# The last four rows of a logsumexp loaded as four uneven runs of columns, with VectorE adding up their parts

## The chip, the cores and the metric

The kernel runs on one core of a Trainium2 chip. The metric is device time in microseconds (us), the median of several runs on the same chip. A profile is one more execution, recorded by the hardware profiler; its times are given from the start of its span.

## The reference

```python
def setup_inputs():
    batch, seq, dim = 32, 512, 1024
    return {
        "x": np.random.randn(batch, seq, dim).astype(np.float32),
        "axis": -1,
    }

def reference(x: np.ndarray, axis: int) -> np.ndarray:
    x_max = np.max(x, axis=axis, keepdims=True)
    return (x_max.squeeze(axis) + np.log(np.sum(np.exp(x - x_max), axis=axis))).astype(np.float32)
```

A logsumexp over the last axis: 16,384 rows of 1024 fp32 numbers (67.1 MB) come in, 16,384 numbers (65.5 KB) go out.

## The kernel before

**Layout.** The 16,384 rows are spread over the 128 partitions, 128 rows to a partition (`x_v`, `NB = 128`); below, "a row" means one row of 1024 columns on every partition, 512 KB in all. A ring of 51 rows in SBUF (`ring`) takes them in.

**Optimistic pass.** The kernel does not subtract the maximum first. It takes exp of the raw numbers, sums each row, takes the logarithm of the sums and stores that. It then counts, with a compare against two bounds (`LOW`, `HIGH`) and two small matmuls over the partitions, whether every sum lay between 1e-18 and 1e18. If one did not, a second pass (`second_pass`, `second_vector`) does the whole work again with the maximum subtracted; with this input it is not entered. So the program ends when the verdict has been read and branched on and both stores of the result have landed (the last wait, on `stored`).

**Loads.** `CHUNKS` lists 17 loads, all issued in order by SyncE (SP) in `load(i)`: 4, 15, 16, 16, 16, 14, 13, 9, 7, 5, 4, 3, 2 rows and then four single rows. I number them from 1. A load into ring slots that were used before waits on counters of VectorE (`dve_done`) and ScalarE (`act_done`) until these slots are free. Load 1 is moved ahead of the opening barrier.

**Work on a load.** Each entry of `CHUNKS` is (rows, rows that VectorE sums, parts, by halves). ScalarE waits for the load, takes exp in place over all rows of a part in one instruction (L235), and VectorE sums them: either with one reduction over the part (L255), or, where `by halves` is set, row by row with `tensor_tensor_reduce` (L242), which adds the right half of the row to the left half and accumulates the sum in the same instruction, so that 512 steps do for 1024 columns. The rows that VectorE does not sum are done by ScalarE alone, one row at a time with `accum_out` (L262): an ACTIVATE and then an instruction that reads the accumulator out.

**The end.** The last four rows (`LATE = 4`) are single loads whose sums ScalarE accumulates into PSUM (`late`; L262 for three of them, L225 for the last). Logarithms (L162) are taken in three goes: 81 rows when load 7 is done, 43 rows just before the last row, and the last four. Two stores follow: 124 columns of the result (L276, 496 bytes to a partition), waiting for the second of these, and 4 columns (L278, 16 bytes), waiting for the third. VectorE takes the maximum and minimum of the first 124 sums (L293, L294), compares them and then the four late sums with the bounds (L283, twice), TensorE counts (L304, L307, 6 columns), VectorE sums the counts into `verdict` (L312), and SyncE, VectorE and ScalarE read it and branch.

**Waits.** An instruction carries one wait of its own. Where the program asks for two before an instruction, the one asked for first stays with it and the other becomes an instruction of its own that only waits, just ahead.

Of the kernel before, what the change touches and what calls it, by code (L numbers as in the profile page):

```python
# [7 lines left out]


CHUNKS = [  # L10
    (4, 4, 1, False), (15, 15, 1, False), (16, 16, 2, False), (16, 16, 2, False),
    (16, 15, 2, False), (14, 14, 2, False), (13, 12, 2, False), (9, 8, 1, False),
    (7, 7, 1, True), (5, 4, 1, True), (4, 3, 1, True), (3, 3, 1, False), (2, 2, 1, True),
    (1, 0, 1, False), (1, 0, 1, False), (1, 0, 1, False), (1, 0, 1, False),
]

CUTS = ()
RING_ROWS = 51


UNEVEN = ()
PARTS = ((0, 128, 2), (1, 128, 4), (3, 128, 8), (7, 64, 8), (71, 128, 8))


LN_AT = 7
LN_LAG = 1


LATE = 4


LOW, HIGH = 1e-18, 1e18
# [6 lines left out]
def kernel(  # L39
# [6 lines left out]
    nc = tc.nc  # L46
    P = nc.NUM_PARTITIONS
# [4 lines left out]
    N, D = x_flat.shape  # L52
    assert N % P == 0
    NB = N // P
    assert sum(r for r, *_ in CHUNKS) == NB
    assert sum(STEPS) == NB

    fp32, bf16, int32 = mybir.dt.float32, mybir.dt.bfloat16, mybir.dt.int32
    Exp = mybir.ActivationFunctionType.Exp
    Ln = mybir.ActivationFunctionType.Ln  # L60
    Alu = mybir.AluOpType
    AX = mybir.AxisListType.X

    x_v = x_flat.rearrange("(p t) d -> p t d", p=P)
    out_v = bass.AP(tensor=out.tensor, offset=out.offset, ap=[[NB, P], [1, NB]])


    assert CHUNKS[-1][0] == 1
    spans = list(zip((0, *CUTS), (*CUTS, D)))
    assert 1 <= len(spans) <= 2  # L70
    n_late = LATE - 1 + len(spans)

    K = 2 + n_late

    ring = nc.alloc_sbuf_tensor("ring", [P, RING_ROWS, D], fp32).ap()
    sums = nc.alloc_sbuf_tensor("sums", [P, NB], fp32).ap()
    res = nc.alloc_sbuf_tensor("res", [P, NB], fp32).ap()
    bounds = nc.alloc_sbuf_tensor("bounds", [P, 2, K], fp32).ap()
    above = nc.alloc_sbuf_tensor("above", [P, 2, K], bf16).ap()
    ends = nc.alloc_sbuf_tensor("ends", [P, 2], fp32).ap()  # L80
    weights = nc.alloc_sbuf_tensor("weights", [P, 2], bf16).ap()
    verdict = nc.alloc_sbuf_tensor("verdict", [1, 1], int32).ap()
    peak = nc.alloc_sbuf_tensor("peak", [P, NB], fp32).ap()
# [1 line left out]
    late = nc.alloc_psum_tensor("late", [P, 512], fp32).ap()  # L85

    ALL_GOOD = P * K
    TOO_MANY = 2048.0
    assert TOO_MANY > ALL_GOOD

    landed = [nc.alloc_semaphore(f"landed{i}") for i in range(len(CHUNKS) + len(spans) - 1)]
    act_done = nc.alloc_semaphore("act_done")
    dve_done = nc.alloc_semaphore("dve_done")
    pool_done = nc.alloc_semaphore("pool_done")
# [22 lines left out]

    place = []
    row = slot = 0
    for r, *_ in CHUNKS:  # L120
        if slot + r > RING_ROWS:
            slot = 0
        place.append((slot, row))
        slot += r
        row += r
# [6 lines left out]
        ends = [-(-n * k // parts) for k in range(parts + 1)]  # L132
        return [(lo, hi) for lo, hi in zip(ends, ends[1:]) if lo < hi]

    def load(i):
        (s, row), r = place[i], CHUNKS[i][0]
        act_wait = max(a for a, _ in busy[s : s + r])
        dve_wait = max(d for _, d in busy[s : s + r])
        if dve_wait:
            nc.sync.wait_ge(dve_done, dve_wait)  # L140
        if act_wait:
            nc.sync.wait_ge(act_done, act_wait)
        dst, src = ring[:, s : s + r], x_v[:, row : row + r]
        if i == len(CHUNKS) - 1:
            for k, (lo, hi) in enumerate(spans):
                nc.sync.dma_start(out=dst[:, :, lo:hi], in_=src[:, :, lo:hi]).then_inc(
                    landed[i + k], 16
                )
        elif i in UNEVEN:
            for first, last, step in PARTS:  # L150
                nc.sync.dma_start(
                    out=dst[first:last:step], in_=src[first:last:step]
                ).then_inc(landed[i], 16)
        else:
            nc.sync.dma_start(out=dst, in_=src).then_inc(landed[i], 16)

    def take_logs(lo, hi, src, dve_wait, act_wait, bias=0.0):
        nonlocal acts
        nc.scalar.wait_ge(act_done, act_wait)
        if dve_wait:  # L160
            nc.scalar.wait_ge(dve_done, dve_wait)
        nc.scalar.activation(out=res[:, lo:hi], in_=src, func=Ln, bias=bias).then_inc(  # L162
            act_done, 1
        )
        acts += 1

    late_row = place[-LATE][1]
    assert not any(n_dve for _, n_dve, _, _ in CHUNKS[-LATE:])

    def total(t):  # L170
        return late[:, t - late_row : t - late_row + 1] if t >= late_row else sums[:, t : t + 1]

    body = nc.main_func.blocks[-1]
    n_barrier = len(body.instructions)
# [33 lines left out]
    nc.gpsimd.memset(weights[:, :1], 1.0)  # L208
    nc.gpsimd.memset(weights[:, 1:], -TOO_MANY).then_inc(pool_done, 1)

    logged = 0
    done_before = [(0, 0)]
    for i, (r, n_dve, parts, by_halves) in enumerate(CHUNKS):
        if i:
            load(i)
        s, row = place[i]
        if i == LN_AT:
            logged = place[i - LN_LAG][1]
            take_logs(0, logged, sums[:, :logged], *done_before[i - LN_LAG])
        if i == len(CHUNKS) - 1:  # L220
            take_logs(logged, late_row, sums[:, logged:late_row], *done_before[-LATE])
            early_logs = acts
            for k, (lo, hi) in enumerate(spans):
                nc.scalar.wait_ge(landed[i + k], 16)
                nc.scalar.activation(  # L225
                    out=ring[:, s, lo:hi],
                    in_=ring[:, s, lo:hi],
                    func=Exp,
                    accum_out=late[:, LATE - 1 + k : LATE + k],
                ).then_inc(act_done, 1)  # L230
                acts += 1
            continue
        nc.scalar.wait_ge(landed[i], 16 * (len(PARTS) if i in UNEVEN else 1))
        for lo, hi in cuts(n_dve, parts):
            nc.scalar.activation(  # L235
                out=ring[:, s + lo : s + hi], in_=ring[:, s + lo : s + hi], func=Exp
            ).then_inc(act_done, 1)
            acts += 1
            nc.vector.wait_ge(act_done, acts)
            if by_halves:  # L240
                for j in range(lo, hi):
                    nc.vector.tensor_tensor_reduce(  # L242
                        out=ring[:, s + j, : D // 2],
                        in0=ring[:, s + j, : D // 2],
                        in1=ring[:, s + j, D // 2 :],
                        scale=1.0,
                        scalar=0.0,
                        op0=Alu.add,
                        op1=Alu.add,
                        accum_out=sums[:, row + j : row + j + 1],  # L250
                    ).then_inc(dve_done, 1)
                    dves += 1
                    busy[s + j] = (0, dves)
            else:
                nc.vector.reduce_sum(  # L255
                    out=sums[:, row + lo : row + hi], in_=ring[:, s + lo : s + hi], axis=AX
                ).then_inc(dve_done, 1)
                dves += 1
                for j in range(lo, hi):
                    busy[s + j] = (0, dves)  # L260
        for j in range(n_dve, r):
            nc.scalar.activation(  # L262
                out=ring[:, s + j],
                in_=ring[:, s + j],
                func=Exp,
                accum_out=total(row + j),
            ).then_inc(act_done, 1)
            acts += 1
            busy[s + j] = (acts, 0)
        done_before.append((dves, acts))  # L270

    take_logs(late_row, NB, late[:, : NB - late_row], dves, acts)


    nc.sync.wait_ge(act_done, early_logs)
    nc.sync.dma_start(out=out_v[:, :late_row], in_=res[:, :late_row]).then_inc(stored, 16)  # L276
    nc.sync.wait_ge(act_done, acts)
    nc.sync.dma_start(out=out_v[:, late_row:], in_=res[:, late_row:]).then_inc(stored, 16)  # L278


    def compare(lo, hi, values):
        nonlocal dves
        nc.vector.tensor_tensor(  # L283
            out=above[:, :, lo:hi],
            in0=values.unsqueeze(1).to_broadcast([P, 2, hi - lo]),
            in1=bounds[:, :, lo:hi],
            op=Alu.is_gt,
        ).then_inc(dve_done, 1)
        dves += 1

    nc.vector.wait_ge(act_done, done_before[-LATE][1])
    nc.vector.wait_ge(dve_done, dves)
    nc.vector.reduce_max(out=ends[:, :1], in_=sums[:, :late_row], axis=AX).then_inc(dve_done, 1)  # L293
    nc.vector.tensor_reduce(  # L294
        out=ends[:, 1:], in_=sums[:, :late_row], axis=AX, op=Alu.min
    ).then_inc(dve_done, 1)
    dves += 2
    nc.vector.wait_ge(pool_done, 1)
    nc.vector.wait_ge(dve_done, dves)
    compare(0, 2, ends)  # L300
    nc.vector.wait_ge(act_done, acts)
    compare(2, K, late[:, :n_late])
    nc.tensor.wait_ge(dve_done, dves)
    nc.tensor.matmul(  # L304
        votes[:1, :K], lhsT=weights[:, :1], rhs=above[:, 0], start=True, stop=False
# [90 lines left out]
```

## Time and profile before

| | us |
|---|---|
| median of 3 runs (lowest, highest) | 162.49 (162.25, 162.52) |
| the profiled execution, its own time | 162.67 |
| span of its trace | 161.3 |
| DVE (VectorE) busy | 121.9 |
| ACT (ScalarE) busy | 115.1 |
| bytes read from HBM | 67.11 MB, 416 GB/s over the span |

The largest groups of instructions, with their number, busy time and mean length:

| line, engine | what | number | busy us | mean ns |
|---|---|---|---|---|
| L255 DVE | sums of a part, one reduction | 14 | 111.2 | 7994 |
| L235 ACT | exp of a part | 18 | 104.4 | 5836 |
| L242 DVE | sum of a row by halves | 16 | 9.9 | 684 |
| L262 ACT | exp and sum of one row | 8 | 8.2 | 1041 |

The engines' busy times are averages over stages with different limits. Two instructions on one engine overlap a little in the trace (the end of one and the start of the next), so the distance from start to start of two that follow each other without a wait is what one costs, and it is a little shorter than the duration shown.

### The profile page before, as it was taken

The page shows a single profiled execution, that of the slowest core. Times are in us where ns is not written, and L with a number is a line of the kernel's source. Part 1 is how long each engine was busy: PE and PEld are TensorE (multiplying, and loading weights), DVE is VectorE, ACT ScalarE, POOL GpSimd, SP SyncE. Part 2 cuts the span into 40 slices and gives each one's busy share as a digit, 9 for nine tenths or more (in the row PEclk, how much of TensorE's full clock was granted, in tenths as well). Part 3 has the DMA queues.
Part 4 walks back from the last instruction along what each step waited for, and adds up shares of the span by engine and source line. Part 5 has one row for each costly group of instructions (what it writes and reads, how often), then busy time and mean ns, then how long its engine had stood idle before and what let it go on. Part 6 is the DMA issues. An engine that isn't in the chain of part 4 may idle for free.

```text
span 161.3 us, 149 instructions
## 1 busy us (share of the span) xinstructions
PE 0.2 (0%) x2; PEld 0.1 (0%) x2; DVE 121.9 (76%) x51; ACT 115.1 (71%) x40; POOL 0.4 (0%) x8
## 2 busy tenths in 40 slices
PE   0000000000000000000000000000000000000000
PEld 0000000000000000000000000000000000000000
DVE  0028000003999999999999699999999999999884
ACT  3170005996079960999419993999199999999996
POOL 1000000000000000000000000000000000000000
DMA  7999799979979989989979999999999999999991
GB/s 256 508 488 442 305 472 520 439 341 520 439 341 520 423 358 520 423 358 520 423 325 455 455 455 439 423 423 423 412 402 430 436 420 410 427 436 412 417 407 42
DMA packets 2737, 67.18 MB, mean 417 GB/s; under 512 B 560, under 2 KB 560, under 8 KB 1072
## 3 DMA queue, kind: packets, MB, share of 16 engines
q1 hardware_dynamic: 2736, 67.18, 97.4%
q14 instruction: 1, 0.01, 0.0%
HBM read 67.11 MB, written 0.07 MB: 416 GB/s over the span
## 4 chain that ended last, share of the span: by engine, by line
DMA 49%; DVE 30%; ACT 20%; issue 0%; PE 0%
DMA ring<-in_x_dram 49%; DVE sums L255 29%; ACT ring L235 17%; ACT ring L262 3%; ACT ring L225 1%; ACT res L162 0%; DVE above L283 0%; PE votes L304 0%; DVE verdict L312 0%; PE votes L307 0%
## 5 line engine op out<-in xcount | busy, mean ns | idle before, releaser
L255 DVE TENSOR_REDUCE sums<-ring 128x8 f32<-128x8192 f32 (+5 forms) x14 | 111.2, 7994 | 37.3 <-ACT ring L235 37.2
L235 ACT ACTIVATE ring<-ring 128x8192 f32<-128x8192 f32 (+6 forms) x18 | 104.4, 5836 | 43.9 <-DMA ring<-in_x_dram 43.9
L242 DVE CUSTOM_DVE_ANT_0 ring<-ring 128x512 f32<-128x512 f32 x16 | 9.9, 684 | 0.0
L262 ACT ACTIVATE ring<-ring 128x1024 f32<-128x1024 f32 x8 | 8.2, 1041 | 0.0
L205 ACT ACT_TABLE_LOAD x1 | 1.3, 1283 | 0.8 <-PEq L377 0.8
L262 ACT ACTIVATION_READ_ACCUMULATOR ring<-ring 128x1 f32 x8 | 1.4, 174 | 0.0
L242 DVE DVE_READ_ACCUMULATOR2_ANT sums<- 128x1 f32 x16 | 1.3, 80 | 0.0
L225 ACT ACTIVATE ring<-ring 128x1024 f32<-128x1024 f32 x1 | 1.0, 1040 | 0.0
L283 DVE TENSOR_TENSOR above<-late,bounds 128x8 bf16<-128x8 f32 x1 | 0.2, 168 | 0.7 <-ACT res L162 0.7
L162 ACT ACTIVATE res<-sums 128x81 f32<-128x81 f32 (+1 forms) x2 | 0.5, 248 | 0.0
L312 DVE TENSOR_REDUCE verdict<-votes 1x1 int32<-1x6 f32 x1 | 0.2, 152 | 0.3 <-PE votes L307 0.3
L293 DVE TENSOR_REDUCE ends<-sums 128x1 f32<-128x124 f32 x1 | 0.3, 282 | 0.1
L304 PE MATMUL votes<-above,weights 128*1 128x6 bf16 x1 | 0.2, 167 | 160.0 <-DVE above L283 160.0
L294 DVE TENSOR_REDUCE ends<-sums 128x1 f32<-128x124 f32 x1 | 0.3, 271 | 0.0
L283 DVE TENSOR_TENSOR above<-ends,bounds 128x4 bf16<-128x4 f32 x1 | 0.2, 162 | 0.1
L162 ACT ACTIVATE res<-late 128x4 f32<-128x4 f32 x1 | 0.2, 173 | 0.0
L304 PEld LDWEIGHTS votes<-above,weights 128*1 128x1 bf16 x1 | 0.1, 80 | 160.0 <-DVE above L283 160.0
L307 PE MATMUL votes<-above,weights 128*1 128x6 bf16 x1 | 0.2, 165 | 0.0
L225 ACT ACTIVATION_READ_ACCUMULATOR ring<-ring 128x1 f32 x1 | 0.2, 153 | 0.0
L206 POOL MEMSET bounds<- 128x6 f32 x1 | 0.1, 104 | 0.4 <-POOLq L377 0.4
L207 POOL MEMSET bounds<- 128x6 f32 x1 | 0.1, 104 | 0.0
L377 POOL MEMSET const-bfloat16-1.0<- 128x1 bf16 x1 | 0.1, 103 | 0.0
(6 smaller groups left out, 0.6 us busy)
## 6 DMA issues: line engine op xcount, KB each, us to landing
ring<-in_x_dram SPq DMA_DIRECT2D x1, 7680.0 KB, 25.1
ring<-in_x_dram SPq DMA_DIRECT2D x1, 7168.0 KB, 28.6
ring<-in_x_dram SPq DMA_DIRECT2D x1, 6656.0 KB, 35.7
ring<-in_x_dram SPq DMA_DIRECT2D x1, 4608.0 KB, 20.3
ring<-in_x_dram SPq DMA_DIRECT2D x2, 2048.0 KB, 16.2
ring<-in_x_dram SPq DMA_DIRECT2D x1, 3584.0 KB, 28.5
ring<-in_x_dram SPq DMA_DIRECT2D x1, 2560.0 KB, 27.5
ring<-in_x_dram SPq DMA_DIRECT2D x4, 512.0 KB, 27.2
```

What stands on the lines that cost most here:

```text
L162: nc.scalar.activation(out=res[:, lo:hi], in_=src, func=Ln, bias=bias).then_inc(act_done, 1)
L205: nc.scalar.preload_act_table_set("natural_log_exp_and_others")
L225: nc.scalar.activation(out=ring[:, s, lo:hi], in_=ring[:, s, lo:hi], func=Exp, accum_out=late[:, LATE - 1 + k : LATE + k],).then_inc(act_d ...
L235: nc.scalar.activation(out=ring[:, s + lo : s + hi], in_=ring[:, s + lo : s + hi], func=Exp).then_inc(act_done, 1)
L242: nc.vector.tensor_tensor_reduce(out=ring[:, s + j, : D // 2], in0=ring[:, s + j, : D // 2], in1=ring[:, s + j, D // 2 :], scale=1.0, scal ...
L255: nc.vector.reduce_sum(out=sums[:, row + lo : row + hi], in_=ring[:, s + lo : s + hi], axis=AX).then_inc(dve_done, 1)
L262: nc.scalar.activation(out=ring[:, s + j], in_=ring[:, s + j], func=Exp, accum_out=total(row + j),).then_inc(act_done, 1)
L283: nc.vector.tensor_tensor(out=above[:, :, lo:hi], in0=values.unsqueeze(1).to_broadcast([P, 2, hi - lo]), in1=bounds[:, :, lo:hi], op=Alu.i ...
L293: nc.vector.reduce_max(out=ends[:, :1], in_=sums[:, :late_row], axis=AX).then_inc(dve_done, 1)
L294: nc.vector.tensor_reduce(out=ends[:, 1:], in_=sums[:, :late_row], axis=AX, op=Alu.min).then_inc(dve_done, 1)
L304: nc.tensor.matmul(votes[:1, :K], lhsT=weights[:, :1], rhs=above[:, 0], start=True, stop=False)
L307: nc.tensor.matmul(votes[:1, :K], lhsT=weights[:, 1:], rhs=above[:, 1], start=False, stop=True).then_inc(counted, 1)
```

## The change

- The loads become 4, 16, 16, 15, 16, 14, 13, 9, 7, 5, 4, 3, 2 rows (the second now has 16 rows and the fourth 15), and then the last four rows, which are taken as one run of 4096 columns to a partition and loaded in pieces of 1600, 1088, 832 and 576 columns (`CUTS`). There are 17 loads as before. Loads 2 and 3 have one exp and one reduction each; before, load 3 had two of each.
- ScalarE takes exp of each piece in one instruction. VectorE sums the first three pieces by halves: for each row, or part of a row, in a piece one `tensor_tensor_reduce` over half its columns. A part of a row that has a sum already takes that sum in as its starting scalar (`scalar=total(row)`) and waits for the instruction that made it. In a piece the part that goes on with an old row comes last, so that no instruction needs two waits. The fourth piece is summed by ScalarE into `late`, and its logarithm takes in the rest of the last row's sum as `bias`.
- Other rows move between the two engines: VectorE sums 14 of 15, 14 of 16, 13 of 14, 12 of 13, 8 of 9, 6 of 7, 2 of 5, 3 of 4, 3 of 3 and 2 of 2 rows of loads 4 to 13, ScalarE the rest. Load 9 (7 rows) is now summed by one reduction and not by halves, load 12 (3 rows) by halves and not by a reduction.
- Logarithms: 67 rows ahead of load 7 (before: 81 rows ahead of load 8), 60 rows at the end, once VectorE's last sum is there, and then the last row alone. Stores: 67 columns after the last load was issued, and 61 columns (244 bytes to a partition) at the end.
- Verdict: maximum and minimum are taken over the 94 rows of loads 1 to 7, right after the first reduction of load 8, into two columns behind `sums`; the other 34 sums and these two are compared one by one (36 columns), the last piece's alone after that. TensorE counts 37 columns, not 6. ScalarE waits once for GpSimd's constants at the start.

```diff
 CHUNKS = [
-    (4, 4, 1, False), (15, 15, 1, False), (16, 16, 2, False), (16, 16, 2, False),
-    (16, 15, 2, False), (14, 14, 2, False), (13, 12, 2, False), (9, 8, 1, False),
-    (7, 7, 1, True), (5, 4, 1, True), (4, 3, 1, True), (3, 3, 1, False), (2, 2, 1, True),
-    (1, 0, 1, False), (1, 0, 1, False), (1, 0, 1, False), (1, 0, 1, False),
+    (4, 4, 1, False), (16, 16, 1, False), (16, 16, 1, False), (15, 14, 2, False),
+    (16, 14, 2, False), (14, 13, 2, False), (13, 12, 2, False), (9, 8, 1, False),
+    (7, 6, 1, False), (5, 2, 1, True), (4, 3, 1, True), (3, 3, 1, True), (2, 2, 1, True),
 ]
-CUTS = ()
+LAST_ROWS = 4
+CUTS = (1600, 2688, 3520)
-LN_AT = 7
-LN_LAG = 1
-LATE = 4
+LOG_AT, LOG_UPTO = 6, 4
+EARLY = 6
...
+    spans = list(zip((0, *CUTS), (*CUTS, LAST_ROWS * D)))
+    early_rows = sum(r for r, *_ in CHUNKS[: EARLY + 1])
+    K = NB - early_rows + 2 + 1
+    all_sums = nc.alloc_sbuf_tensor("sums", [P, NB + 2], fp32).ap()
+    sums = all_sums[:, :NB]
...
+    def take_logs(lo, hi, src, dve_wait, act_wait, bias=0.0, dve_last=False):
         nonlocal acts
-        nc.scalar.wait_ge(act_done, act_wait)
-        if dve_wait:
-            nc.scalar.wait_ge(dve_done, dve_wait)
+        waits = [(dve_done, dve_wait), (act_done, act_wait)]
+        for sem, value in waits if dve_last else reversed(waits):
+            nc.scalar.wait_ge(sem, value)
...
+    def halves(s, row, lo=0, hi=D):
+        nonlocal dves
+        half = (hi - lo) // 2
+        nc.vector.tensor_tensor_reduce(
+            out=ring[:, s, lo : lo + half],
+            in0=ring[:, s, lo : lo + half],
+            in1=ring[:, s, lo + half : hi],
+            scale=1.0,
+            scalar=total(row) if lo else 0.0,
+            op0=Alu.add,
+            op1=Alu.add,
+            accum_out=total(row),
+        ).then_inc(dve_done, 1)
+        dves += 1
+        parts_done[row] = dves
...
+                if i == EARLY + 1 and not lo:
+                    nc.vector.wait_ge(dve_done, done_after[EARLY][0])
+                    for k, op in enumerate((Alu.max, Alu.min)):
+                        nc.vector.tensor_reduce(
+                            out=all_sums[:, NB + k : NB + k + 1],
+                            in_=sums[:, :early_rows],
+                            axis=AX,
+                            op=op,
+                        ).then_inc(dve_done, 1)
+                        dves += 1
...
+    s, row = place[-1]
+    wait_free(s, LAST_ROWS)
+    here, there = flat(ring[:, s : s + LAST_ROWS]), flat(x_v[:, row:])
+    for k, (lo, hi) in enumerate(spans):
+        nc.sync.dma_start(out=here[:, lo:hi], in_=there[:, lo:hi]).then_inc(
+            landed[len(CHUNKS) + k], 16
+        )
+
+    nc.sync.wait_ge(act_done, logs_done)
+    nc.sync.dma_start(out=out_v[:, :logged], in_=res[:, :logged]).then_inc(stored, 16)
+    for k, (lo, hi) in enumerate(spans):
+        last = k == len(spans) - 1
+        nc.scalar.wait_ge(landed[len(CHUNKS) + k], 16)
+        nc.scalar.activation(
+            out=here[:, lo:hi],
+            in_=here[:, lo:hi],
+            func=Exp,
+            accum_out=late[:, :1] if last else None,
+        ).then_inc(act_done, 1)
+        acts += 1
+        if not last:
+            rows = list(range(lo // D, -(-hi // D)))
+            if lo % D:
+                rows = rows[1:] + rows[:1]
+            nc.vector.wait_ge(act_done, acts)
+            for j in rows:
+                if row + j in parts_done:
+                    nc.vector.wait_ge(dve_done, parts_done[row + j])
+                halves(s + j, row + j, max(lo - j * D, 0), min(hi - j * D, D))
+    summed = acts
...
+    take_logs(logged, NB - 1, sums[:, logged : NB - 1], dves, done_after[-1][1], dve_last=True)
+    take_logs(NB - 1, NB, late[:, :1], parts_done[NB - 1], summed, bias=total(NB - 1))
     nc.sync.wait_ge(act_done, acts)
-    nc.sync.dma_start(out=out_v[:, late_row:], in_=res[:, late_row:]).then_inc(stored, 16)
+    nc.sync.dma_start(out=out_v[:, logged:], in_=res[:, logged:]).then_inc(stored, 16)
...
+    compare(above[:, :, : K - 1], all_sums[:, early_rows:])
     nc.vector.wait_ge(act_done, acts)
-    compare(2, K, late[:, :n_late])
+    compare(above[:, :, K - 1 :], late[:, :1])
```

## The prediction

> **What bounds the kernel now.** I read the slices and the queue table of the page first, then the chain of waits, then the timeline of the last 9 us, then single groups for their costs.
>
> ```profile
> DMA  7999799979979989989979999999999999999991
> ...
> q1 hardware_dynamic: 2736, 67.18, 97.4%
> ```
>
> The sixteen DMA engines are busy in every slice but the last, 97.4% of the span. The chain alternates between loads and the engines that free ring slots:
>
> ```profile
> 31 pieces in order of time: start us, us, what
> ...
> 38.91 16.16 DVE sums L255
> ...
> 55.09 28.82 DMA ring<-in_x_dram
> ...
> 90.99 31.28 DVE sums L255 x4
> ...
> 122.29 24.89 DMA ring<-in_x_dram
> ...
> 147.19 2.76 ACT ring L235
> ```
>
> That would suggest VectorE as a bound, but a load issued at 55.09 or 122.29 only joins a queue that is still full: the loads ahead of it landed at 64.56 and 142.28. The landings, from the trace's semaphore records, follow without a gap: loads 4 to 13 at 64.56, 83.91, 100.85, 116.59, 127.53, 136.22, 142.28, 147.17, 150.86 and 153.35, the single rows at 154.62, 155.90, 157.18 and 158.42. A 16-row load takes 19.35 us (83.91 less 64.56), one row 1.28. So the stream of loads sets 158.42, and the timeline shows what lies behind it:
>
> ```profile
> 157.35 1.05 ACT L262 ACTIVATE ring<-ring 128x1024 f32<-128x1024 f32 x1
> ...
> 157.56 0.69 DVE L242 CUSTOM_DVE_ANT_0 ring<-ring 128x512 f32<-128x512 f32 x1
> ...
> 158.30 0.16 ACT L262 ACTIVATION_READ_ACCUMULATOR ring<-ring 128x1 f32 x1
> 158.35 0.24 ACT L162 ACTIVATE res<-sums 128x43 f32<-128x43 f32 x1
> ...
> 158.49 1.04 ACT L225 ACTIVATE ring<-ring 128x1024 f32<-128x1024 f32 x1
> ...
> 159.44 0.15 ACT L225 ACTIVATION_READ_ACCUMULATOR ring<-ring 128x1 f32 x1
> 159.62 0.17 ACT L162 ACTIVATE res<-late 128x4 f32<-128x4 f32 x1
> 159.82 0.34 SPq L278 DMA_DIRECT2D out_dram<-res  x1
> ...
> 160.28 0.15 DVE L312 TENSOR_REDUCE verdict<-votes 1x1 int32<-1x6 f32 x1 [0.28 <-PE votes L307]
> ```
>
> ScalarE starts the last row 0.07 after it landed (it was finishing the 43 logarithms), and the last logarithm ends at 159.79. Two things run from there: the store (issued 159.82, landed 161.23, so 1.41) and the verdict (to 160.43, then reading and branching until 161.21). Both end within 0.03 us of each other; the span is 161.29.
>
> **Prices, all from this trace.** ScalarE, start to start: 7168 columns 6.08, 3072 columns 2.65, 2048 columns 1.80, so 0.833 ns a column and 0.093 an instruction (1600 columns 1.43, 1088 1.00, 832 0.79, 576 0.57). A row with its sum read out costs 1.04 into SBUF (149.86 to 150.90). VectorE: reductions of 8, 7 and 6 rows 8.59, 7.53, 6.46; a row by halves 0.61 for 512 steps. At 1.04 ns a step (1.067 us a row in the reductions) that is 0.08 and the steps, so 320 steps 0.41, 288 0.38, 224 0.31, 192 0.28. These smaller ones are not in the trace: a flat 0.61 each would be the upper bound, the steps alone the lower; I take the straight line, since 6, 7 and 8 rows lie on one.
>
> **Loads.** Same bytes, same 17 loads. Packets of 4096 bytes took 159 ns and of 8192 bytes 309, so 9 ns a packet and the rest by bytes; 6400, 4352, 3328 and 2304 bytes sum to what four of 4096 do. The stream's end stays at 158.42, provided that it never runs dry. The second load of 16 rows makes it come nearer: load 2 lands about 1.2 later, 27.06, its exp (13.85) and reduction (17.2) end at 58.2 instead of 55.06, and load 5 is issued there, 6.3 us ahead of 64.56 where it was 9.5. The single reduction of load 3 ends at 77.5 and lets load 6 go, 6.4 ahead of 83.91. The first packet of a store came 0.85 after its issue, so some 5 us of queued work still hide it: nothing. The exp and reductions of loads 4 to 8 are hidden by the same queue; so are the wait for GpSimd's constants (set by 1.00, first exp at 7.54) and the early maximum and minimum, unless VectorE is late below. The 67-column store is issued near 130.5, behind the loads, with 28 us to land.
>
> **ScalarE's tail.** Load 9 lands at 136.22 and its exp starts at 136.24, as before. From there: 6 rows 5.23 and one row 1.04, to 142.51 (load 10 landed 142.28); 2 rows 1.80 and three rows 3.12, to 147.43; 3 rows 2.65 and one row 1.04, to 151.12; 2.65, to 153.77; 1.80, to 155.57; the pieces 1.43, 1.00, 0.79, starting at 155.57, 157.00, 158.00 and 158.79. By bytes the pieces land at 155.31, 156.66, 157.71 and 158.42. So ScalarE is 0.2 to 0.4 behind all the way and never waits; it now sums one row more in load 9 and two more in load 10 by itself, at 1.04 instead of 0.83. The last piece is done at 159.51 and the engine is free at 159.41, where before the last sum was out at 159.59.
>
> **VectorE's tail.** It ends load 7 at 134.88, waits for the exp of load 8 (135.10), 8.59 to 143.73, maximum and minimum 0.16 each (0.20 for 124 columns now), 6 rows 6.46 to 150.51, two halves to 151.73, three to 153.57, waits for 153.87, three to 155.74, two to 156.96. First piece ready 157.09: 0.61 and 0.38, to 158.12. Second ready 158.09: 0.41 and 0.31, to 158.85. Third ready 158.88: 0.31 and 0.28, to 159.50, its accumulator read 0.08 later, 159.58. The added waits on VectorE's own earlier sum are for instructions done 0.3 or more before, so they hold nothing; behind them stand only the next sums.
>
> **The new wait at the end.** The 60 logarithms wait for that last sum: 159.62, not 159.41. Behind them in ScalarE's queue stands the last row's logarithm, for which the store and the last compare wait. 60 logarithms cost 0.14 (60 columns by the line above); the last row's starts at 159.76 and ends, by its 0.17, at 159.93. Before: 159.79. **+0.14.**
>
> **Unknown: the scalar operand.** Two sums take a starting value from SBUF; no row of VectorE has that. Between 0 and 0.08 each (what one more read instruction costs here); a gain has no mechanism. I take 0.04 each; the first disappears in 0.06 of slack (158.85 to 158.91). **+0.04.**
>
> **Store and verdict.** 16 bytes a partition landed in 1.41, 496 bytes in 1.55 on fifteen of sixteen engines (the page's 2.2 is the sixteenth). 244 bytes between them: 1.48, **+0.07** (0 to 0.14). The verdict gets 31 columns more in two matmuls and a reduction, about 0.05, which lies beside the store. The 36-column compare starts at 159.63 and is over before the last logarithm.
>
> Sum: +0.25 on a span of 161.29, so 161.54; this execution's own 162.67 becomes 162.92. That execution is 0.18 above the median of the runs, so the median goes from 162.49 to **162.74**. Two tenths of a per cent, 0.32 us, is about what this measurement tells from no change; the sum falls just inside it.
>
> **Rivals.**
>
> (a) *A block of code meets the last store.* The page's queue table has one more packet:
>
> ```profile
> q14 instruction: 1, 0.01, 0.0%
> ```
>
> It is 8192 bytes, moved from 159.51 to 160.11 on one engine; the sixteenth part of the 124-column store waited behind it (fifteen landed by 160.16, it at 160.85, so up to 0.7), for nothing, because nobody needed that store then. If it is fetched when VectorE reaches a certain instruction, that place (the maximum, minimum and first compare, 158.4 to 158.9, just ahead of its end) is reached in the changed kernel only after 159.6, so the packet comes near 160.4 to 160.8, and the 61-column store's packets, 0.85 behind its issue at 159.96, come at 160.8. From a start after 160.2 on (0.6 ahead of 160.8) a part of the store lands later, up to 0.7, with nothing behind which to hide: 0.35 as the middle, 163.1. Against: if ScalarE or SyncE fetches it, it falls among the loads, where 0.3 on one engine mostly disappears. The Trainium skill ("Runtime: NRT & Kernel Launch", Instruction fetch mechanics) says that code is prefetched by the sequencer and that crossing a block is mostly hidden; by that rule this rival is nothing and the sum stands. The trace bears it out only for a store that nobody waited for.
>
> (b) *The short last piece pays in full.* If ScalarE is not behind, the last piece starts at 158.43, its sum is out at 159.16 and its logarithm ends at 159.36: 0.43 sooner, less 0.07 for the store, 162.1. For it: the loads are spaced by bytes so that each exp ends as the next piece lands. Against: the sum of the steps above has ScalarE behind from 142.5 on, and VectorE's chain alone ends at 159.58.
>
> (c) *VectorE is not late.* If its short sums cost the steps alone (0.08 less each, two in the third piece), the logarithms start at 159.45 and the end stays within 0.1 of before: 162.5.
>
> (d) *The loads run dry.* If a load needs more than 6.3 us from issue to first packet, or the odd sizes move slower, the stream's end moves with it; 0.5 to 1 us, 163.3. Against: 0.85 for the store, and 2736 packets with hardly a gap.
>
> **Chances.** The sum as it is, 162.55 to 162.95: 0.45, a third of it above 162.81 for the noise of the runs and the upper bounds. (a) 0.23, all slower. (b) 0.12, faster. (c) 0.12, no difference. (d) 0.08, slower. So faster 0.12, same 0.30 + 0.12 = 0.42, slower 0.15 + 0.23 + 0.08 = 0.46. The likeliest single case is the sum, 162.74, its own range 162.55 to 162.95. The range of 8 in 10 takes in (c) and most of (a), and leaves out (b) and the far end of (d): 162.35 to 163.25.
>
> **What would show it.** In the profile after: the last piece's exp starting near 158.8 and not at its landing near 158.4 (wrong for (b)); no idle time ahead of ScalarE's exps from load 10 on; the 60 logarithms starting 0.03 after VectorE's last accumulator read, near 159.6; the distance between the sums with a scalar operand against the line; the instruction packet's time against the last store's landing; landings of loads 5 and 6 still at 83.9 and 100.9. A stream ending 0.2 or more away from 158.4, or a last logarithm outside 159.7 to 160.1, makes the sum wrong.

## The result, and the profile after

| | before | after |
|---|---|---|
| median of the runs, us | 162.52 | 163.59 |
| lowest, highest | 162.25, 162.74 | 163.28, 163.81 |
| ratio, 95% interval | | 1.0064 [1.0054, 1.0074] |
| the profiled execution, its own time | 162.67 | 163.42 |
| span of its trace | 161.29 | 162.04 |
| last load landed | 158.42 | 158.24 |
| last logarithm ended | 159.79 | 159.88 |
| last store issued, landed | 159.82, 161.23 | 159.90, 162.01 |

The changed kernel is 1.07 us slower: four times the sum that was forecast, and above the range's upper end (163.25). The loads are not the reason, and the engines hardly are: the last logarithm ends 0.08 us later. The last store, issued 0.08 us later, lands 0.78 us later.

The tail of the changed kernel, from its timeline (start, length, engine, line, instruction; in brackets the idle time just before and what ended it):

```profile
158.70 0.39 DVE L205 CUSTOM_DVE_ANT_0 ring<-ring 128x224 f32<-128x224 f32 x1
...
159.01 0.41 DVE L205 CUSTOM_DVE_ANT_0 ring<-ring,sums 128x192 f32<-128x192 f32 x1
159.14 0.16 ACT L295 ACTIVATION_READ_ACCUMULATOR ring<-ring 128x1 f32 x1
159.35 0.08 DVE L205 DVE_READ_ACCUMULATOR2_ANT sums<- 128x1 f32 x1
159.47 0.26 ACT L151 ACTIVATE res<-sums 128x60 f32<-128x60 f32 x1 [0.18 <-DVE sums L205]
...
159.63 0.25 ACT L151 ACTIVATE res<-late,sums 128x1 f32<-128x1 f32 x1
159.90 0.34 SPq L318 DMA_DIRECT2D out_dram<-res  x1
...
160.48 0.18 DVE L334 TENSOR_REDUCE verdict<-votes 1x1 int32<-1x37 f32 x1 [0.31 <-PE votes L329]
```

ScalarE's last piece is summed at 159.30, the 60 logarithms wait 0.18 us for VectorE's last sum, and the last row's stands behind them: the chain is the forecast one. Then SyncE's waits, longest first (waiter, releaser, us in total, times, longest):

```profile
SPq L318 <- ACT res L151: 22.3, 1, 22.3
...
SPq L371 <- SPq L371: 0.6, 1, 0.6
SPq L338 <- DVE verdict L334: 0.4, 1, 0.4
```

L371 is the last wait of the program, the one for the stores; the kernel before has no such line. The store's issue and landing, by the instructions that write the result:

```profile
L318 SPq DMA_DIRECT2D out_dram<-res x1: 343/343/343, 159.9 to 159.9; - x1
...
DMA to landing us min/median/max: 2.1/15.1/28.1
```

2.1 us from issue to landing where the forecast had 1.48. Fifteen of its sixteen parts did land by 161.37, which is 1.47; the sixteenth came at 162.01. The DMA engines between 160.6 and 161.2 show what stood in front of it:

```profile
DMA  0000900000345689976655432100000000000001
GB/s 0 0 0 0 546 0 0 0 0 16 81 114 130 130 179 260 212 131 147 130 130 98 82 49 49 17 0 0 0 0 0 0 0 0 0 0 0 0 0 33
...
q1 hardware_dynamic: 137, 0.03, 23.7%
q14 instruction: 1, 0.01, 5.5%
```

One packet of code (q14) starts at 160.66, the store's packets from 160.74 on. By the trace's own records the code packet holds its engine from 160.663 to 161.188; the eight packets of the store on that engine run from 161.185 to 161.301, where the others are through by 161.01. In the kernel before the packet came at 159.51 and met the first store. This is rival (a).

### The profile page after: what moved, and what is told of

Same layout as the page of the kernel before. It is cut to its first block, busy times and chain, and to the rows that moved or that the text cites. A ratio compares the mean times of both kernels' runs of the same rounds, so it can differ in the third digit from the quotient of the medians.

```text
span 162.0 us, 157 instructions
## 1 busy us (share of the span) xinstructions
PE 0.2 (0%) x2; PEld 0.1 (0%) x2; DVE 120.8 (75%) x50; ACT 115.9 (72%) x48; POOL 0.5 (0%) x8
## 4 chain that ended last, share of the span: by engine, by line
DMA 47%; ACT 34%; DVE 17%; issue 0%; SPq 0%; PE 0%
DMA ring<-in_x_dram 47%; ACT ring L244 28%; DVE sums L254 15%; ACT ring L272 4%; DVE ring L205 2%; ACT ring L295 1%; SPq L140 0%; ACT res L151 0%; PE votes L326 0%; DVE verdict L334 0%; DVE above L222 0%; DVE sums L205 0%; PE votes L329 0%
## 5 line engine op out<-in xcount | busy, mean ns | idle before, releaser
L254 DVE TENSOR_REDUCE sums<-ring 128x7 f32<-128x7168 f32 (+4 forms) x13 | 111.2, 8599 | 39.2 <-ACT ring L244 39.2
L244 ACT ACTIVATE ring<-ring 128x7168 f32<-128x7168 f32 (+6 forms) x17 | 99.3, 5869 | 43.0 <-DMA ring<-in_x_dram 43.0
L272 ACT ACTIVATE ring<-ring 128x1024 f32<-128x1024 f32 x11 | 11.5, 1044 | 0.0
L205 DVE CUSTOM_DVE_ANT_0 ring<-ring 128x512 f32<-128x512 f32 (+3 forms) x14 | 8.2, 637 | 0.1
L295 ACT ACTIVATE ring<-ring 128x1600 f32<-128x1600 f32 (+3 forms) x4 | 3.9, 1048 | 0.0
L272 ACT ACTIVATION_READ_ACCUMULATOR ring<-ring 128x1 f32 x11 | 2.1, 191 | 0.0
L205 DVE CUSTOM_DVE_ANT_0 ring<-ring,sums 128x224 f32<-128x224 f32 (+1 forms) x2 | 0.9, 432 | 0.0
L151 ACT ACTIVATE res<-sums 128x67 f32<-128x67 f32 (+1 forms) x2 | 0.5, 250 | 0.2 <-DVE sums L205 0.2
L295 ACT ACTIVATION_READ_ACCUMULATOR ring<-ring 128x1 f32 x1 | 0.2, 158 | 0.0
```

Of the source, the lines that this page charges most:

```text
L205: nc.vector.tensor_tensor_reduce(out=ring[:, s, lo : lo + half], in0=ring[:, s, lo : lo + half], in1=ring[:, s, lo + half : hi], scale=1.0 ...
L244: nc.scalar.activation(out=ring[:, s + lo : s + hi], in_=ring[:, s + lo : s + hi], func=Exp).then_inc(act_done, 1)
L254: nc.vector.reduce_sum(out=sums[:, row + lo : row + hi], in_=ring[:, s + lo : s + hi], axis=AX).then_inc(dve_done, 1)
L272: nc.scalar.activation(out=ring[:, s + j], in_=ring[:, s + j], func=Exp, accum_out=total(row + j),).then_inc(act_done, 1)
L295: nc.scalar.activation(out=here[:, lo:hi], in_=here[:, lo:hi], func=Exp, accum_out=late[:, :1] if last else None,).then_inc(act_done, 1)
```

## The experiments

All are timed against the kernel before on the same chip. The first group asks whose code it is and whether it is the cause. An added wait below is one that was long satisfied; two of them make one instruction.

**e1_vector8, e2_scalar8, e3_sync8: eight more instructions on one engine.**

```diff
         s, row = place[i]
+        if i == 4:
+            for _ in range(16):
+                nc.vector.wait_ge(act_done, 1)
```

(e2: `nc.scalar.wait_ge(pool_done, 1)`; e3: `nc.sync.wait_ge(dve_done, 1)`.)

> The changed kernel with eight more instructions in VectorE's stream, waits that are long satisfied, ahead of its work on load 5. In the changed kernel's profile the 8192-byte instruction packet runs from 160.66 to 161.19 us, in front of one sixteenth of the last store, which lands at 162.01 where the other fifteen land by 161.37. Theory A (the block of code is fetched when VectorE reaches a certain place in its program): the place comes eight instructions sooner, the packet near 159.0 to 159.5, the last store lands whole by about 161.4, the span falls from 162.04 to about 161.5 and the time by 0.5 us, to about 1.003 of the kernel before. Rival B (another engine's code, or a fetch at a fixed time): packet and time as in the changed kernel, 1.006.

> The changed kernel with the same eight satisfied waits in ScalarE's stream, ahead of its work on load 5. Theory A: the packet stays at 160.66 and the time at 1.006 of the kernel before. Rival B1 (ScalarE's code): the packet comes some 3 us sooner, among the loads, and the time falls by 0.5 us.

> The changed kernel with the same eight satisfied waits in SyncE's stream, after load 5 is issued. Theory A: the packet stays at 160.66 and the time at 1.006 of the kernel before. Rival B2 (SyncE's code): the packet moves away from the last store, to about 130 us or out of the program, and the time falls by 0.5 us.

**e4_before_vector8:** the same eight on VectorE in the kernel before.

> The kernel before with the same eight waits in VectorE's stream. Theory A: the packet, at 159.51 there, comes sooner by the time of eight instructions (2 to 6 us: 153 to 157), among the loads or ahead of the first store; the time stays within 0.2% of the kernel before, since nothing waits for the first store. Should the time fall by more than 0.3 us, the packet cost the kernel before something too.

What was measured, with the later kernels of this group; packet times are from the trace's records of the queue of instruction packets. The time outside the span is an execution's own time less the span of its recorded work, the median over the runs:

| kernel | code packet | last load landed | last store: 15 of 16, all | outside span | ratio to before [95%] |
|---|---|---|---|---|---|
| before | 159.51 to 160.11 | 158.42 | 161.20, 161.23 | 1.36 | 1 |
| after | 160.66 to 161.19 | 158.24 | 161.37, 162.01 | 1.39 | 1.0064 [1.0054, 1.0074] |
| e2_scalar8 | 160.33 to 160.76 | 157.93 | 161.01, 161.67 | 1.39 | 1.0056 [1.0040, 1.0072] |
| e3_sync8 | 160.34 to 160.96 | 157.94 | 161.04, 161.95 | 1.38 | 1.0075 [1.0055, 1.0096] |
| e1_vector8 | 154.13 to 154.46 | 158.34 | 161.21, 161.24 | 1.51 | 1.0051 [1.0037, 1.0066] |
| g1_vector2 | 157.02 to 157.34 | 157.84 | 160.92, 160.94 | 1.48 | 1.0028 [1.0017, 1.0038] |
| h1_dead4 | 157.21 to 157.53 | 158.14 | 161.23, 161.25 | 1.48 | 1.0024 [1.0015, 1.0032] |
| f1_code_behind | behind the span | 158.01 | 161.07, 161.10 | 1.91 | 1.0038 [1.0022, 1.0054] |
| h4_dead_less4 | behind the span | 158.41 | 161.49, 161.52 | 1.85 | 1.0056 [1.0039, 1.0074] |
| e4_before_vector8 | 147.22 to 147.55 | 158.53 | 161.31, 161.34 | 1.38 | 1.0028 [1.0016, 1.0040] |
| h2_before_dead_less2 | 159.68 to 160.12 | 157.97 | 160.79, 161.04 | 1.36 | 1.0016 [1.0007, 1.0026] |
| h3_before_dead_less4 | 159.74 to 160.27 | 157.97 | 160.79, 161.12 | 1.34 | 1.0029 [1.0015, 1.0043] |
| f2_before_code_behind | behind the span | 158.06 | 160.83, 160.87 | 1.91 | 1.0027 [1.0015, 1.0039] |

Only VectorE's instructions move the packet: measured from the landing of the last load, it comes 2.42 us later in the changed kernel, 2.40 in e2 and e3, and 4.21 sooner in e1. So it is VectorE's code. With e1 the store lands whole, as expected, but the time falls by 0.1 to 0.2% only (the intervals overlap), not by 0.5 us. The packet had come 6.5 us sooner, not 1.5, and lay among the loads: behind load 13 the four pieces land 1.96, 1.71, 1.05 and 0.69 apart, where the changed kernel has 1.95, 1.39, 1.03 and 0.71, so the slowest engine lost 0.3 us. The time outside the span is longer, too. e4 misses its expectation, and its trace shows the same loss: load 12 lands 4.33 behind load 11 (before: 3.69), the later loads keep that delay, and the time goes up by 0.28%.

**f1_code_behind, f2_before_code_behind: VectorE's part of the second pass, eleven instructions that stand ahead of its first pass in memory, moved behind it.**

```diff
-    nc.br("first_pass", engines=vector)
-    with nc.body("second_vector", valid_engines=vector):
-        ...
-    nc.switch_bb("first_pass")
...
+    with nc.body("second_vector", valid_engines=vector):
+        ...
     nc.switch_bb("last", parent=opening)
```

> The changed kernel with VectorE's eleven instructions of the second pass moved from ahead of its first pass to behind it, so that VectorE's program up to the verdict is twelve instructions shorter; nothing that runs is changed but one branch at the start. Theory A (the block of code is fetched when VectorE reaches a certain place): the place is not reached before the program ends, no instruction packet lies in the span, the last store lands whole about 1.47 us after its issue, and what is left of the slowdown is the forecast's sum, +0.25 us: 1.001 to 1.002 of the kernel before. Rival (the packet is not the cause, or something else makes up the difference): 1.005 to 1.007 as before.

> The kernel before with the same eleven instructions moved behind its first pass. Theory A: its packet at 159.51 only met the first store, for which nobody waits; without it the time stays the same, 0.999 to 1.001.

In the span both come out as expected: f1 161.1 (median of its runs) against 161.0 for the kernel before, f2 160.9. In time both miss: 1.0038 and 1.0027. The time outside the span went from 1.39 to 1.91 in both: the packets now start 1.0 us behind the last recorded instruction (f1: 162.17 against 161.17). That the program's end waits for them is an inference; all five kernels with VectorE's code there (f1 to f4, h4) have 1.85 to 1.93. That the code is moved out of the span does not make it free.

**g1_vector2: two more instructions on VectorE** (as e1, with `range(4)`).

> The changed kernel with two more instructions in VectorE's stream (satisfied waits, ahead of its work on load 5), and its code otherwise where it was. Eight of them brought the instruction packet from 160.66 to 154.13, into the loads, where it held one engine's loads up by about 0.4 us; moving the code away altogether gave the span 0.9 us but added 0.5 us outside it. Theory A (the packet in front of the last store is most of the loss): with two the packet comes between 158.4 and 160.1, behind the loads and ahead of the last store, holds up nothing, the last store lands whole, the time outside the span stays 1.38, and the time is the forecast's sum, 1.001 to 1.003 of the kernel before. Rival E (the instructions added cost as much as they save, or the loss lies elsewhere): 1.005 or more.

1.0028: most of the loss is gone, the store is whole, and at 157.02 the packet holds up no load that one can see (the last pieces land 1.39, 1.02 and 0.72 apart, the last at 157.84). Two things differ from what was expected: the packet came in the loads' last 0.8 us, not behind them, and the time outside the span is 0.13 us longer than that of the kernel before.

**g2_before_three_fewer: the kernel before with three VectorE instructions fewer.**

```diff
-    (7, 7, 1, True), (5, 4, 1, True), (4, 3, 1, True), (3, 3, 1, False), (2, 2, 1, True),
+    (7, 7, 1, True), (5, 4, 1, True), (4, 3, 1, True), (3, 3, 1, False), (2, 2, 1, False),
```

> The kernel before with the two rows of load 13 summed by one reduction in place of two sums by halves: three instructions fewer in VectorE's stream. By the durations VectorE is done with it at 159.1, not 158.2, and with the first compare at 159.7, still ahead of the last logarithm at 159.79, so the engines alone would leave the time within 0.1 us. Theory A: the packet comes later by three instructions, from 159.51 to between 160.2 and 161, and if it starts before 160.7 it stands in front of one sixteenth of the last store: 0.3 to 0.6 us slower, 1.002 to 1.004. If it starts after 160.9 the store is whole and the time unchanged.

1.0087 [1.0070, 1.0105]: more than twice what was expected. The packet came at 160.84, and one part of the last store landed late (162.26, the others by 161.83: 0.43). The rest is a wait that the expectation forgot; from its timeline:

```profile
158.93 0.24 ACT L162 ACTIVATE res<-sums 128x43 f32<-128x43 f32 x1 [0.86 <-DVE sums L255]
...
159.08 1.04 ACT L225 ACTIVATE ring<-ring 128x1024 f32<-128x1024 f32 x1
```

VectorE ends load 13 at 158.84; the 43 logarithms wait for it, and the last row's exp, whose data landed at 158.05, stands behind them. It starts 1.03 us after its data landed, where the kernel before has 0.07: 0.96 us lost, 0.86 of it idle. So g2 says little of the packet alone; it does show what a late VectorE costs when ScalarE's queue stands behind its sums.

**h1_dead4, h2_before_dead_less2, h3_before_dead_less4, h4_dead_less4: nothing that runs is changed.** VectorE's part of the second pass lies ahead of its first pass in memory and is jumped over. These four make it longer or shorter.

```diff
+        for _ in range(8):
+            nc.vector.wait_ge(dve_again, 1)
         nc.vector.wait_ge(act_again, len(steps) + 1)
```

(h1. For h2 the last `reduce_sum` and the `tensor_add` are left out, for h3 and h4 all of the third step and the `tensor_add`.)

> The changed kernel with four more instructions in VectorE's part of the second pass, which stands in memory ahead of its first pass and isn't entered with this input: nothing that runs is changed, only the place of VectorE's code in memory. Theory A: the instruction packet comes sooner, as with two or eight instructions that run (157.0 and 154.1), and the last store lands whole; 1.001 to 1.004 of the kernel before, 0.4 to 0.7 us faster than the changed kernel. Rival E (the packet's place has no part in it): 1.006 as in the changed kernel.

> The kernel before with the last two of VectorE's eleven instructions of the second pass left out (the last sum and the addition of the maximum; not entered with this input). Nothing that runs is changed. Theory A: the packet, at 159.51 in the kernel before, comes later; if it starts between 160.1 and 160.7 it stands in front of a part of the last store and the kernel before becomes 0.3 to 0.7 us slower, 1.002 to 1.004; otherwise the time stays. Rival E: the time stays wherever the packet comes.

> As h2_before_dead_less2 with four instructions left out (all of the second pass's third step and the addition). Theory A: the packet comes later still; in front of the last store (starting between 160.1 and 160.7) 1.002 to 1.004, behind it (from 160.9) as the kernel before, unless the program's end waits for it.

> The changed kernel with the same four instructions left out of the second pass, which isn't entered. Theory A: the packet comes later than 160.66; behind the last store's packets (from 160.9) the store lands whole and the time falls below the changed kernel's 1.006, to 1.002 to 1.004, unless the program's end waits for the block. Rival E: 1.006.

These settle the cause. Four instructions that never run, added to the changed kernel, take 0.4% off its time (1.0064 to 1.0024, intervals apart); SyncE's waits in h1 no longer have one for the stores at the end (with two lines more in the kernel that would be L373; L371 is here the wait ahead of it), and the store takes 1.4 us:

```profile
SPq L320 <- ACT res L151: 22.3, 1, 22.3
...
SPq L340 <- DVE verdict L336: 0.3, 1, 0.3
SPq L371 <- DVEq L340: 0.2, 1, 0.2
```

```profile
L320 SPq DMA_DIRECT2D out_dram<-res x1: 343/343/343, 159.8 to 159.8; - x1
...
DMA to landing us min/median/max: 1.4/14.8/28.1
```

Instructions that never run, taken out of the kernel before, make it slower, and its last wait shows why; SyncE's waits of h3:

```profile
SPq L278 <- ACT res L162: 0.8, 1, 0.8
SPq L349 <- SPq L349: 0.4, 1, 0.4
SPq L316 <- DVE verdict L312: 0.3, 1, 0.3
```

L349 is there the last wait, for the stores. The times, 1.0016 and 1.0029, are near what was expected of a packet in front of the store, but that was to start after 160.1. It came at 159.68 (h2) and 159.74 (h3), where the expectation of h2 lets it hold up nothing. It was through at 160.12 in h2, 0.09 ahead of the store's first packet, and at 160.27 in h3, 0.07 behind the first of them. Still one part of the store landed 0.25 and 0.33 behind the other fifteen.

The six traces with a late part of the last store have something in common. The part lands 0.82 (after), 0.91 (e2), 0.99 (e3), 0.85 (g2), 0.92 (h2) and 0.85 us (h3) behind the end of the code packet. So it is late even where the code no longer holds its engine (h2). In the kernel before, 0.99 behind the packet's end would be 161.10, ahead of the 161.23 at which the store lands in any case. Why it takes so long is open.

In h4 the store is whole, but the packets come behind the end and the time outside the span is 1.85: 1.0056, the exception that its expectation named. Its time alone would not tell it from rival E; its store does.

The second group asks what the rest is.

**f3_even: cuts at 1024, 2048 and 3200** (and the code behind, as f1).

```diff
-CUTS = (1600, 2688, 3520)
+CUTS = (1024, 2048, 3200)
```

> As f1_code_behind, with the last four rows cut at 1024, 2048 and 3200 columns in place of 1600, 2688 and 3520: two whole rows, a row and an eighth, 896 columns. Theory C (the rest of the loss is VectorE's last sum, on which the 60 logarithms and behind them the last row's wait): by the steps in the traces the third piece's sums end near 159.2 and the last row's logarithm ends near 159.65, where the changed kernel has 159.88; the time falls 0.2 us below f1_code_behind, to 1.000 of the kernel before. Rival D (ScalarE, 0.3 behind the loads, sets the end whatever the cuts): as f1_code_behind.

**f4_last_row_first and g4_last_row_first_vector2: the last row's logarithm first** (f4 with the code behind as f1, g4 with two more instructions as g1).

```diff
-    take_logs(logged, NB - 1, sums[:, logged : NB - 1], dves, done_after[-1][1], dve_last=True)
     take_logs(NB - 1, NB, late[:, :1], parts_done[NB - 1], summed, bias=total(NB - 1))
+    take_logs(logged, NB - 1, sums[:, logged : NB - 1], dves, done_after[-1][1], dve_last=True)
```

> As f1_code_behind, with the last row's logarithm taken ahead of the 60 others, so that it no longer stands behind the wait for VectorE's last sum. Theory C: it starts 0.03 after its own sum is out, the 60 follow at VectorE's last sum, the later of both ends 0.1 to 0.15 us sooner than in f1_code_behind, and so does the program. Rival D: no change.

> As g1_vector2, with the last row's logarithm taken ahead of the 60 others. Theory C (the last row's logarithm stands behind a wait for VectorE's last sum): the later of the two logarithms ends 0.14 us sooner than in g1_vector2, and the time is lower by about that, 1.000 to 1.002 of the kernel before.

In the traces theory C (VectorE's last sum, and the two logarithms behind it) holds. From the landing of the last load to the end of the last logarithm it takes 1.61 us in f1, 1.46 in f3 and 1.49 in f4; in the kernel before 1.37. From the timeline of g4:

```profile
158.85 0.15 ACT L298 ACTIVATION_READ_ACCUMULATOR ring<-ring 128x1 f32 x1
159.03 0.26 ACT L151 ACTIVATE res<-late,sums 128x1 f32<-128x1 f32 x1
159.06 0.08 DVE L205 DVE_READ_ACCUMULATOR2_ANT sums<- 128x1 f32 x1
159.19 0.24 ACT L151 ACTIVATE res<-sums 128x60 f32<-128x60 f32 x1
```

The last row's logarithm starts ahead of VectorE's read-out, not behind it. In the times it does not come out of the noise: g4 1.0018 [1.0007, 1.0029] beside g1's 1.0028 [1.0017, 1.0038], f3 1.0049 [1.0032, 1.0067] and f4 1.0036 [1.0023, 1.0049] beside f1's 1.0038 [1.0022, 1.0054]. A gain of 0.15 us is 0.09%, and the intervals reach 0.10 to 0.18% to either side. f3 was expected at 1.000 and misses.

**g5_loads_as_before_vector2: the loads before** (as g1).

```diff
-    (4, 4, 1, False), (16, 16, 1, False), (16, 16, 1, False), (15, 14, 2, False),
+    (4, 4, 1, False), (15, 15, 1, False), (16, 16, 2, False), (16, 15, 2, False),
```

> As g1_vector2, with loads 2 to 4 as in the kernel before (15, 16, 16 rows, loads 3 and 4 in two parts). The forecast costs the 16 rows in the second load at nothing: same landings from load 5 on within 0.1 us, same time as g1_vector2 within 0.1%. Rival: load 5 is issued 3 us sooner and the time falls by more than 0.2 us.

The 16 rows in the second load cost nothing that the trace shows: load 5 lands at 83.70 in g5 and 83.52 in g1, load 6 at 100.61 and 100.41, spans 161.2 and 161.1. That is more than the 0.1 us expected, but the whole of g5's trace is later: load 1 lands there at 7.47, in g1 at 7.31. The time is 1.0036 [1.0022, 1.0050] of the kernel before, not below g1's 1.0028, so the rival is out. By the medians g5 is 0.16% above g1, more than the 0.1% expected, but the intervals overlap. The time outside the span is 1.63, not 1.48. VectorE has one instruction more in g5; why the end takes longer was not settled.

No version of the changed kernel beat the kernel before; the nearest was g4.

## Why the prediction was wrong

- *What bounds the kernel* stood: the loads land without a gap in both, at 158.42 and 158.24 the last, and the odd sizes cost what the bytes said (pieces 1.95, 1.39, 1.03 and 0.71 apart; forecast 1.96, 1.35, 1.05, 0.71). Rival (d) is out.
- *ScalarE's tail* stood to 0.01 us from its start on: that start was at 136.03, 0.21 sooner than costed, with load 9 landed at 135.99 in this execution. The third piece's exp ended at 158.67, 0.21 ahead of the forecast's 158.88. Rival (b) is out; ScalarE never waited again.
- *VectorE's short sums* lie on the line: 0.38 for 288 steps, 0.42 for 320, 0.31 for 224. Rival (c) is out. *The scalar operand*, taken at 0.04, costs 0.06: 0.372 for 224 steps with it and 0.314 without. (The one with it also carries a wait for VectorE's own earlier sum; the two were not separated.) The forecast's times for VectorE are 0.03 to 0.04 above its own terms behind each wait (157.09, 0.61 and 0.38 make 158.08, not 158.12); the trace has 0.02 there.
- *The new wait at the end* was there and was mis-sized by 0.10: the 60 logarithms cost 0.16, not 0.14, and the last row's 0.25, not 0.17. The last row's has a bias out of SBUF, where the row that I priced it by (four logarithms out of PSUM) has a constant one; that this is the reason was not tested.
- *The store* whole: 1.47 measured, 1.48 forecast.
- With all these the program would have ended near 161.49 in this execution (its verdict was through at 161.43, and the last wait took 0.06 more in the kernel before); the forecast's sum ended at 161.54. g1 (two satisfied waits more) and h1 (nothing more that runs), where the packet is out of the store's way, show that sum in the runs: spans 0.2 us above those of the kernel before, 1.0028 and 1.0024 of its time. Of their 0.4 us, 0.13 lies outside the span, which the sum did not have. A second instruction packet comes there at 161.99 (g1) and 162.46 (h1), none in the kernel before. The changed kernel has it too, at 162.49, but with 1.39 outside the span, as before: the packet comes 1.83 us behind the end of the verdict's sum in both the changed kernel and g1, and where the store is late most of that passes inside the span. So this part of the loss shows only once the store lands whole. Whose code it is, and that it costs the 0.13, was not tested.
- **The step that failed** is the one that gave VectorE's code block no term in the sum, because in the kernel before it cost nothing. It was written down as rival (a), with the right packet, the right engine's code and the right victim, at a chance of 0.23, and at a price of 0.35 us that was too small. The runs show a price of 0.55 in the profiled execution (162.04 less 161.49) and of 0.6 us between the changed kernel and g1 or h1 (0.36 to 0.40%). The code's time on its engine does not give that price by itself: the store's packets behind it start 0.44 late (161.185 against 160.74), and their part lands 0.64 late.
- That the packet came at 160.66, within the 160.4 to 160.8 of rival (a), is in part luck. The rival had it fetched when VectorE reaches a certain instruction near its end. By that rule two instructions more move it by two instructions, and the last two compares in the changed kernel start at 159.55 and 160.00. In g1 it came 0.82 us ahead of the last load's landing, where the changed kernel has it 2.42 behind.
- The rule of the Trainium skill that was set against it ("Runtime: NRT & Kernel Launch", Instruction fetch mechanics: code is prefetched, crossing a block is mostly hidden) holds for VectorE here: its list of waits has none for code, and from the end of the verdict's sum to the end of its branch it takes 0.72 us in both kernels. It doesn't hold for the DMA engine that carries the block: 0.53 us of it, in front of the last store. Here the measurement decides.

## What to carry to other kernels

Here the program's code travelled over the DMA engines that carry its data. Where the end hangs on one small store, look in the records of the instruction queue for a packet near it, before and after every change of the program; a change of 0.4% can be nothing but that, and a few instructions that never run are enough to test it. And a short last piece can only pay if the engine that takes it isn't behind by then: here ScalarE started 0.2 to 0.4 us behind the landing of every load from load 10 on (load 10 landed at 142.08, its exp started at 142.28; the last piece at 158.24 and 158.56). No run here took that delay away.

## What the hardware showed that I had not expected

- The place of the packet is not proportional to the number of instructions. Measured from the landing of the last load, two more on VectorE brought it from 2.42 us behind to 0.82 ahead, eight to 4.21 ahead; four that never run, to 0.93 ahead. What sets it stayed open.
- A packet that ends before the store's packets come can still cost: in h2 by 0.25 us, with the code through at 160.12 and the store's first packet at 160.21.
- A code packet among the loads can cost, though the loads are queued far ahead: e1 and e4 lost 0.3 to 0.6 us on the slowest engine, for a packet of 0.33 us. The prediction had such a packet mostly disappear; in g1 and h1, where it came within 1 us of the loads' end, it did.
- Code that is wanted only behind the last recorded instruction goes with a longer program all the same: 1.91 us outside the span in f1 and f2, 1.39 in the kernel before.
- The store issued behind seventeen loads (L291) kept SyncE's queue for 7.21 us, where the four issues just ahead of it took 0.33 to 0.47. Here nothing stood behind it.
